# Two zero products over all 128 rows ahead of each group of 32-row merging products in a hybrid HGRN2 / RWKV-7 step

## The chip, the cores and the metric

The kernel runs on one core of a Trainium2 chip. The metric is the device time of one execution in microseconds (us); a smaller number is better. The core's engines are TensorE (PE in the profile, with its weight loads as PEld), VectorE (DVE), ScalarE (ACT), GpSimd (POOL) and SyncE (SP), which issues most of the DMAs.

## The reference

One inference step of a two-layer trunk: layer 0 is an HGRN2 mixer, layer 1 is an RWKV-7 mixer, each beside cross-attention to a memory, with a gate, an output projection and a residual. 1024 prompt tokens and 8 sequences of 8 sample tokens go through. What the change touches is the recurrence of RWKV-7:

```
def step(S, inp):
    r_t, w_t, k_t, v_t, a_t, b_t = inp
    sa = jnp.einsum('bhij,bhj->bhi', S, a_t)
    S = S * w_t[:, :, None, :] + sa[..., None] * b_t[:, :, None, :] + v_t[..., None] * k_t[:, :, None, :]
    y = jnp.einsum('bhij,bhj->bhi', S, r_t)
    return S, y
```

There are 16 heads of width 64, and everything is computed in 32-bit floating point.

## The kernel before, in words

The recurrence is computed in chunks of 64 tokens. A block (class `Blk`) holds 128 tokens of the prompt, that is two chunks (`E` = 2), or the 64 sample tokens (`E` = 1). There are eight prompt blocks and one sample block, in the order 0, sample, 1, 2, ... 7 (`RSEQ`). For a chunk and a head the feedback through `sa` is a unit triangular system of 64 rows, and its inverse is built in these steps:

- `pre` loads and scales the operands (tiles `BKz`, `AR`, `G`).
- `score` forms 64x64 tables of all heads on TensorE (tile `psc`, L1461) and VectorE writes them, masked, to `Q` (L1464).
- `inverse` solves blocks of 16 rows on VectorE, one row after another (tiles `pd` and `Xc`, L1534 and L1535).
- `merge_steps` puts the 16-row blocks together to 32 rows and these to 64 rows, by products of 32x32 matrices on TensorE (all in L1560). This is where the change is.
- `chain` carries the state from chunk to chunk (tiles `chain` and `chainS`, L1643 to L1700), and `out` normalizes and stores.

In `merge_steps` the inner function `prods` makes five steps: `pn1`, `px32`, `py32`, `pn2`, `py64` (the profile and the orders print them as `pn`, `px`, `py`, `pn`, `py`, with the operands behind the arrow). A step works on the quarters of a block, a quarter being 32 rows of one chunk. It takes two quarters at a time: a group. Each quarter of a group has a PSUM bank of its own, from the pool `psi` with two banks, and 16 products of 32x32 (one for each head) fill the bank; the two quarters alternate in the code, and an engine then copies the 32 filled rows out of the bank. `pn1` and `py32` have two groups in a prompt block, the others one: seven groups. In the sample block five groups stand, two of them with two quarters and three with one. A 32-bit product shows as two records in the profile, so a group of 32 products has 64 records. A group uses 32 rows and 32 columns of the array at a time.

The order on each engine is not the order of the code. A scheduler places each instruction by a simulated timeline, so that one added instruction can move others on every engine; `chain` stands under `tc.high_priority()`. Merging products of one block therefore lie among the chain of the block ahead of it, the scores (`psc`) of the next one, and the sample block's own work: transposes of its states (`ps`, L1602), products with them (`pas`, L1617), and their addition to the chain (L1647). `chain` already has two products of zeros of the kind that the change adds, in the first block alone (`zb`, L1643, 128 rows, 512 columns, bfloat16).

Of the kernel before, what the change touches and what calls it, by code (L numbers as in the profile page):

```python
# [906 lines left out]
def rwkv_masks(g, rc, c):  # L907

    nc = g.nc
    BF16 = mybir.dt.bfloat16  # L910
    si = c.tile([128, 64], I32, name="rsi")
    ti = c.tile([128, 64], I32, name="rti")
    xi = c.tile([128, 64], I32, name="rxi")
    nc.gpsimd.iota(si, pattern=[[0, 64]], base=0, channel_multiplier=1)
    nc.gpsimd.iota(ti, pattern=[[1, 64]], base=0, channel_multiplier=0)
    nc.vector.tensor_scalar(si, si, 63, None, op0=ALU.bitwise_and)
    nc.vector.tensor_tensor(xi, si, ti, op=ALU.bitwise_xor)
    m = g.rmask = rc.tile([128, 2, 128], F32, name="rm")
    for e in range(2):
        nc.vector.tensor_tensor(m[:, e, 64 - 64 * e:128 - 64 * e], ti, si, op=ALU.is_gt)  # L920
        nc.vector.tensor_tensor(m[:, e, 64 * e:64 * e + 64], ti, si, op=ALU.is_ge)
    b = c.tile([128, 64], F32, name="rb")
    nc.vector.tensor_scalar(b, xi, LS, None, op0=ALU.is_lt)
    g.rmask_s = rc.tile([128, 128], F32, name="rms")
    nc.vector.tensor_tensor(g.rmask_s.rearrange("p (a t) -> p a t", a=2), m[:, 0].rearrange("p (a t) -> p a t", a=2),
                            b[:, None, :].to_broadcast([128, 2, 64]), op=ALU.mult)

    g.smask = rc.tile([128, 512], BF16, name="smask")
    nc.vector.memset(g.smask, 1.0)
    nc.vector.memset(g.smask[:, 0:512:64], 0.0)  # L930
    g.smask_s = rc.tile([128, 256], BF16, name="smask_s")
    nc.vector.memset(g.smask_s, 1.0)
    nc.vector.memset(g.smask_s[:, 0:256:LS], 0.0)

    g.BKz = [rc.tile([128, 2, 4, 4, 64], F32, name=f"BKz{k}") for k in range(2)]
    for k in range(2):
        for h in range(2):
            nc.gpsimd.memset(g.BKz[k][HV[1 - h], h], 0.0)

    g.Xc = rc.tile([128, 16, 16], F32, name="Xc")  # L940
    nc.vector.memset(g.Xc, 0.0)
    nc.vector.memset(g.Xc.rearrange("p r t -> p (r t)")[:, 0:256:17], 1.0)
    g.N1p = rc.tile([128, 16, 32], F32, name="N1p")
    for q in range(4):
        s = slice(32 * q, 32 * q + 32)
        nc.vector.tensor_copy(g.N1p[s], g.ident[s, None, s].to_broadcast([32, 16, 32]))
    g.m16 = rc.tile([128, 32], I32, name="m16")
    nc.gpsimd.iota(g.m16, pattern=[[0, 32]], base=0, channel_multiplier=1)
    nc.vector.tensor_scalar(g.m16, g.m16, 16, 4, op0=ALU.bitwise_and, op1=ALU.logical_shift_right)
    g.bm = rc.tile([128, 2], F32, name="bm")  # L950
    nc.vector.tensor_copy(g.bm[:, 1:2], g.m16[:, 0:1])
    nc.vector.tensor_scalar(g.bm[:, 0:1], g.bm[:, 1:2], -1.0, 1.0, op0=ALU.mult, op1=ALU.add)
    nc.vector.memset(g.m16[:, 16:], 0)
# [19 lines left out]
def rwkv_layer(ctx, g, nn, left):  # L973
# [219 lines left out]
    with pool(g, "rtmp", 1) as tmp:  # L1193
        rwkv_masks(g, P["s"], tmp)
# [98 lines left out]
def copy(nc, eng, dst, src):  # L1293
    if eng == "scalar":
        nc.scalar.activation(dst, src, AF.Copy)
    else:
        getattr(nc, eng).tensor_copy(dst, src)
# [67 lines left out]
class Blk:  # L1365
# [179 lines left out]
    def merge_steps(self):  # L1545

        g, Q, XN, XP = self.g, self.Q, self.XN, self.XP
        nc = g.nc
        quart, un, ac = self.quart, self.un, self.ac
        XM = self.tile("XM", "XM", 16, 32)  # L1550
        N1 = g.N1p
        tl = lambda nm: g.psi.tile([128, 16, 32], F32, name=nm, tag="i")

        def prods(nm, qs, out, lhs, rhs, evac):

            for k in range(0, len(qs), 2):
                zs = [(c, tl(nm)) for c in qs[k:k + 2]]
                for u in range(16):
                    for c, z in zs:
                        nc.tensor.matmul(z[out(*c), u], lhs(u, *c), rhs(u, *c), start=True, stop=True)  # L1560
                for c, z in zs:
                    evac(z[out(*c)], *c)

        def to_q(z, e, s, c):
            for k in range(2):
                nc.scalar.activation(un(k, e, s, c), z[:, 8 * k:8 * k + 8], AF.Copy)
        Qu = lambda u, e, s, o: Q[u // 8][s, self.turn(e, u // 8), u % 8 // 4, u % 4, ac(e, o, 32)]
        same = lambda e, q, s: s
        order = [c for c in quart if c[1] == 0] + [c for c in quart if c[1] == 1]
        lo = [c for c in quart if c[1] == 0]  # L1570
        up = lambda s: slice(s.start + 32, s.stop + 32)
        prods("pn1", order, same, lambda u, e, q, s: Qu(u, e, s, 32 * q), lambda u, e, q, s: XN[s, u],
              lambda z, e, q, s: nc.vector.copy_predicated(N1[s], g.m16[s, None, :].to_broadcast([32, 16, 32]), z))
        yield
        prods("px32", lo, same, lambda u, e, q, s: XP[s, u], lambda u, e, q, s: N1[s, u],
              lambda z, e, q, s: copy(nc, ENG["xm"], XM[s], z))
        yield
        prods("py32", order, same, lambda u, e, q, s: N1[s, u], lambda u, e, q, s: XP[s, u],
              lambda z, e, q, s: to_q(z, e, s, ac(e, 32 * q, 32)))
        yield  # L1580
        prods("pn2", lo, lambda e, q, s: up(s), lambda u, e, q, s: Qu(u, e, s, 32), lambda u, e, q, s: XM[s, u],
              lambda z, e, q, s: copy(nc, ENG["xm"], XM[up(s)], z))
        yield
        prods("py64", lo, same, lambda u, e, q, s: XM[up(s), u], lambda u, e, q, s: Qu(u, e, up(s), 32),
              lambda z, e, q, s: to_q(z, e, s, ac(e, 32, 32)))
# [175 lines left out]
    def out(self, last=False):  # L1761

        for k in range(2):
            self.out_group(k, last)
# [88 lines left out]
```

## Time and profile before

| what | us |
|---|---|
| median of the 3 runs | 2386.9 (2386.75 to 2400.98) |
| the profiled execution's own time | 2401.76 |
| its span, first to last instruction | 2399.8 |
| TensorE matmul busy | 2238.2 (93%) |
| VectorE busy | 1332.2 (56%) |
| ScalarE busy | 1004.3 (42%) |
| GpSimd busy | 717.7 (30%) |

Busy time of TensorE is modelled, since matmuls are pipelined: a product's duration reaches past the start of the next one, and the distance from start to start is what a product takes of the engine. The mean granted TensorE clock was 0.934 of full speed in the profiled execution. The merging products of this program start at 1723.6 us and end at 2210 us of the span; the gate projections before them and the output projection behind them are large products. The profiled execution was as long as the slowest of the three runs.

### The profile page before, as it was taken

The page shows a single profiled execution, that of the slowest core. Times are in us where ns is not written, and L with a number is a line of the kernel's source. Part 1 is how long each engine was busy: PE and PEld are TensorE (multiplying, and loading weights), DVE is VectorE, ACT ScalarE, POOL GpSimd, SP SyncE. Part 2 cuts the span into 40 slices and gives each one's busy share as a digit, 9 for nine tenths or more (in the row PEclk, how much of TensorE's full clock was granted, in tenths as well). Part 3 has the DMA queues.
Part 4 walks back from the last instruction along what each step waited for, and adds up shares of the span by engine and source line. Part 5 has one row for each costly group of instructions (what it writes and reads, how often), then busy time and mean ns, then how long its engine had stood idle before and what let it go on. Part 6 is the DMA issues. An engine that isn't in the chain of part 4 may idle for free. (4 is left out here: it accounts for less than half of the span.)

```text
span 2399.8 us, 50625 instructions
## 1 busy us (share of the span) xinstructions
PE 2238.2 (93%) x20980; PEld 2001.5 (83%) x20981; DVE 1332.2 (56%) x2678; ACT 1004.3 (42%) x2240; POOL 717.7 (30%) x559
## 2 busy tenths in 40 slices
PE   5988999999999979989989998999999998899997
PEld 5988888888788858878979998898889987788786
DVE  6113566556775553365796214245576589874643
ACT  4222444444444442266554313344544455444421
POOL 2123121122112310034553412113143255444432
PEclk9998999999999989999999998999986798887999
DMA  5334111223432264215434425145332233312653
GB/s 184 86 96 142 48 56 45 67 70 91 111 87 87 80 193 127 84 41 199 148 122 163 127 93 145 50 103 134 113 108 72 57 101 99 90 55 82 201 158 105
DMA packets 360312, 252.99 MB, mean 105 GB/s; under 512 B 120379, under 2 KB 326403, under 8 KB 360083
## 3 DMA queue, kind: packets, MB, share of 16 engines
q1 hardware_dynamic: 348034, 237.66, 33.3%
q0 software_dynamic: 2544, 7.64, 0.9%
q10 hardware_dynamic: 9504, 4.46, 0.7%
q8 instruction: 165, 2.70, 0.5%
q14 instruction: 65, 0.52, 0.1%
HBM read 172.59 MB, written 77.11 MB: 104 GB/s over the span
## 5 line engine op out<-in xcount | busy, mean ns | idle before, releaser
L200 POOL TENSOR_TENSOR wlo<-wraw,whi 128x1024 fp32r<-128x1024 f32 (+1 forms) x84 | 214.9, 2560 | 646.5 <-ACT whi L197 623.8
L216 PE MATMUL pg<-hi,whi 128*128 128x288 f32 (+3 forms) x800 | 269.1, 336 | 4.5 <-DVE qk L597 2.3
L218 PE MATMUL pg<-hi,wlo 128*128 128x288 f32 (+3 forms) x800 | 266.0, 333 | 0.0
L217 PE MATMUL pg<-lo,whi 128*128 128x288 f32 (+3 forms) x800 | 265.9, 332 | 0.0
L197 ACT ACTIVATE whi<-wraw 128x1024 fp32r<-128x1024 f32 (+1 forms) x92 | 101.0, 1099 | 178.5 <-issue 104.9
L216 PEld LDWEIGHTS pg<-hi,whi 128*128 128x128 f32 x800 | 153.8, 192 | 21.5 <-issue 4.4
L217 PEld LDWEIGHTS pg<-lo,whi 128*128 128x128 f32 x800 | 153.7, 192 | 12.9 <-issue 3.1
L218 PEld LDWEIGHTS pg<-hi,wlo 128*128 128x128 f32 x800 | 153.5, 192 | 11.8 <-issue 2.3
L890 PE MATMUL pout<-owh,bh 128*128 128x512 f32 (+1 forms) x432 | 143.1, 397 | 9.2 <-ACT owh L197 9.2
L890 PE MATMUL pout<-owl,bh 128*128 128x512 f32 (+1 forms) x432 | 142.0, 394 | 0.1
L890 PE MATMUL pout<-owh,bl 128*128 128x512 f32 (+1 forms) x432 | 141.2, 394 | 0.9 <-DVE bl L200 0.9
L216 PE MATMUL pg<-xhi,whi 128*128 128x384 f32 (+2 forms) x392 | 127.6, 325 | 7.1 <-DVE evs L1136 5.0
L218 PE MATMUL pg<-xhi,wlo 128*128 128x384 f32 (+2 forms) x392 | 126.4, 322 | 0.0
L217 PE MATMUL pg<-xlo,whi 128*128 128x384 f32 (+2 forms) x392 | 125.5, 320 | 0.0
L1461 PE MATMUL psc<-AR,BKz 128*128 128x128 f32 x544 | 98.2, 342 | 17.2 <-DVE Q L1464 9.3
L1461 PEld LDWEIGHTS psc<-AR,BKz 128*128 128x128 f32 x544 | 86.7, 244 | 23.1 <-DVE Q L1464 11.0
L890 PEld LDWEIGHTS pout<-owh,bh 128*128 128x128 f32 (+1 forms) x432 | 78.9, 183 | 31.3 <-ACT owh L197 10.8
L197 ACT ACTIVATE bh<-br 128x512 fp32r<-128x512 f32 (+1 forms) x54 | 32.4, 606 | 171.5 <-POOL br L859 84.4
L200 DVE TENSOR_TENSOR bl<-br,bh 128x512 fp32r<-128x512 f32 (+1 forms) x54 | 49.6, 919 | 96.2 <-ACT bh L197 96.2
L890 PEld LDWEIGHTS pout<-owh,bl 128*128 128x128 f32 (+1 forms) x432 | 78.6, 182 | 22.8 <-DVE bl L200 1.8
L242 PE MATMUL pg<-xhi,wlo 128*128 128x384 f32 (+1 forms) x408 | 96.6, 334 | 0.0
L890 PEld LDWEIGHTS pout<-owl,bh 128*128 128x128 f32 (+1 forms) x432 | 78.8, 183 | 21.1 <-DVE owl L200 0.6
(460 smaller groups left out, 6114.9 us busy)
## 6 DMA issues: line engine op xcount, KB each, us to landing
wraw<-in_w_in_dram SPq DMA_DIRECT2D x72, 512.0 KB
oraw<-in_w_out_dram SPq DMA_DIRECT2D x24, 512.0 KB
wraw<-in_w_mem_kv_dram SPq DMA_DIRECT2D x16, 512.0 KB
gT<-evs SPq DMA_DIRECT2D x12, 544.0 KB
vv<-vtk SPq DMA_DIRECT2D x24, 256.0 KB
br<-brT SPq DMA_DIRECT2D x24, 256.0 KB
br<-mixT SPq DMA_DIRECT2D x24, 256.0 KB
gt<-gT SPq DMA_DIRECT2D x24, 256.0 KB
```

The source lines that it names most:

```text
L197: nc.scalar.activation(hi, src, AF.Copy)
L200: (nc.gpsimd if elo == "pool" else nc.vector).tensor_sub(lo, src, hi.bitcast(F32))
L216: nc.tensor.matmul(out, ah, bh, start=first, stop=False)
L217: nc.tensor.matmul(out, ah, bl, start=False, stop=False)
L218: nc.tensor.matmul(out, al, bh, start=False, stop=last)
L242: nc.tensor.matmul(z[:, :n], a[:, k], x(k)[:, t0:t0 + n], start=first, stop=last)
L890: nc.tensor.matmul(ps[c][:p], a[:, k, :p], w[:, 512 * c:512 * c + 512], start=first, stop=last)
L1461: nc.tensor.matmul(ps[:, j], two(BK[:, h, j, 2 * e:2 * e + 2]), two(AR[:, j, 2 * e:2 * e + 2]), start=True, stop=True)
```

## The change

A tile of 128x128 bfloat16 zeros (`zd`) is made once, in `rwkv_masks`. In `prods`, ahead of the products of a group, each bank of the group gets one product of zeros by zeros over 128 rows, 128 columns of the array and 512 columns of the moving operand, which fills the whole bank with zeros. The merging products then write their 32 rows of the bank as before (`start=True`), so what is copied out of the bank is the same.

```
@@ -919,6 +919,8 @@
         nc.vector.tensor_tensor(m[:, e, 64 * e:64 * e + 64], ti, si, op=ALU.is_ge)
+    g.zd = rc.tile([128, 128], BF16, name="zd")
+    nc.vector.memset(g.zd, 0.0)
     b = c.tile([128, 64], F32, name="rb")
@@ -1555,6 +1557,10 @@
             for k in range(0, len(qs), 2):
                 zs = [(c, tl(nm)) for c in qs[k:k + 2]]
+
+                for _, z in zs:
+                    nc.tensor.matmul(z.rearrange("p u t -> p (u t)"), g.zd, g.zd[:, None, :].to_broadcast([128, 4, 128]),
+                                     start=True, stop=True)
                 for u in range(16):
                     for c, z in zs:
                         nc.tensor.matmul(z[out(*c), u], lhs(u, *c), rhs(u, *c), start=True, stop=True)
```

In the changed program lines behind the first insertion are 2 higher and those behind the second 6 higher: the merging products are L1566 there and the zeros L1562.

The scheduler's order on TensorE in the first prompt block, before: the last half of step `pn2` (`pn<-XM,Q`) and step `py64` (`py<-Q,XM`), a number behind a tile telling one bank from another.

```order
L1560 MATMUL pn_17450<-XM,Q 32x32 x7
L1643 LDWEIGHTS zb
L1643 MATMUL chain_18180<-zb 128x512
L1560 MATMUL pn_17450<-XM,Q 32x32 x9
L1560 MATMUL pn_17451<-XM,Q 32x32 x16
L1560 MATMUL py_17486<-Q,XM 32x32 x16
L1560 MATMUL py_17487<-Q,XM 32x32 x16
L1461 MATMUL psc<-AR,BKz_15166 128x128 x8
```

The same place in the changed program:

```order
L1562 LDWEIGHTS zd
L1562 MATMUL pn_17462<-zd 128x512
L1566 MATMUL pn_17462<-XM,Q 32x32 x16
L1562 LDWEIGHTS zd
L1562 MATMUL pn_17463<-zd 128x512
L1566 MATMUL pn_17463<-XM,Q 32x32 x16
L1491 MATMUL pbk<-ident,BKz_15167 128x64 x4
L1491 MATMUL pbk<-ident,BKz_15168 128x64 x4
L1608 MATMUL ps_18365<-ident,Sn_18366 128x64 x4
L1562 LDWEIGHTS zd
L1562 MATMUL py_17500<-zd 128x512
L1566 MATMUL py_17500<-Q,XM 32x32 x16
```

The second bank's zeros stand behind the first bank's 16 products, not ahead of the group, and transposes (`pbk`, `ps`) that stood elsewhere have come between the two steps. The zeros of the chain (`zb`) have moved to an earlier place.

The second place is the sample block's step `px32` (one bank) on TensorE and what follows it, before:

```order
L1461 MATMUL psc<-AR,BKz_15166 128x128 x4
L1489 MATMUL pbk<-ident,BKz_15165 128x64 x8
L1560 MATMUL px_18870<-N1p,XP 32x32 x16
L1560 MATMUL py_18900<-XP,N1p 32x32 x16
L1647 MATMUL chain_18179<-ident,AS_18347 128x64
L1617 MATMUL pas<-AR,S0T 64x2x8 x8
```

And in the changed program:

```order
L1463 MATMUL psc<-AR,BKz_15167 128x128
L1562 LDWEIGHTS zd
L1562 MATMUL px_18888<-zd 128x512
L1566 MATMUL px_18888<-N1p,XP 32x32 x4
L1653 MATMUL chain_18195<-ident,AS_18363 128x64
L1623 MATMUL pas<-AR,S0T 64x2x8 x8
L1566 MATMUL px_18888<-N1p,XP 32x32 x12
L1463 MATMUL psc<-AR,BKz_15167 128x128 x8
```

The step is cut in two by a round of the sample block's state products, and eight score products follow where the next merging step stood.

## Rows read from the trace of the kernel before

**Rows 1.** The page: busy time of TensorE, and its granted clock in 40 slices.
```profile
PE 2238.2 (93%) x20980; PEld 2001.5 (83%) x20981; DVE 1332.2 (56%) x2678; ACT 1004.3 (42%) x2240; POOL 717.7 (30%) x559
...
PEclk9998999999999989999999998999986798887999
```
**Rows 2.** Busy time by stretch (us): span:, length, engines, PEclk, DMA share, GB/s.
```profile
1786.00:1896.00 110.00, 109.39 (x1261) 102.19 (x1262) 60.21 (x119) 47.48 (x115) 27.76 (x26) 0.57 0.24 62
1896.00:2050.00 154.00, 141.66 (x2456) 126.19 (x2453) 135.63 (x243) 76.01 (x195) 91.82 (x92) 0.92 0.36 96
2050.00:2215.00 165.00, 156.26 (x2570) 140.95 (x2570) 111.72 (x226) 77.29 (x200) 72.77 (x76) 0.82 0.24 69
1723.00:2215.00 492.00, 467.78 (x7249) 425.47 (x7247) 347.58 (x663) 229.06 (x572) 216.99 (x223) 0.81 0.30 81
```
**Rows 3.** The chain that ended last, by line, in 1786:1896 and in 1896:2050.
```profile
by line: PE psc L1461 24.4%; PE pas L1617 18.4%; PE py L1560 14.6%; PE pn L1560 10.4%; PE chain L1647 6.2%; PE pbk L1489 5.6%; PE chain L1652 5.1%; PE px L1560 5.1%; PE ps L1602 3.5%; PE chain L1677 2.5%; PE chain L1650 1.5%; PE chain L1691
...
by line: DVE pd L1534 12.1%; DVE BKz L1425 6.2%; PE chain L1650 6.2%; PE psc L1461 5.9%; DVE G L1415 5.7%; PE chain L1652 5.0%; issue 4.6%; PE chain L1677 4.1%; DVE Xc L1535 3.8%; PE pn L1560 3.6%; PE py L1560 3.6%; PE px L1560 3.4%; DVE UV
```
**Rows 4.** Windows of L1560 alone: PE and PEld busy, PEclk, DMA.
```profile
1723.00:2215.00 492.00, 137.45 (x3808) 124.99 (x3808) 0.81 0.30 81
```
**Rows 5.** TensorE in order of time: start, duration, line, tiles, count.
```profile
1742.64 1.85 PE L1560 MATMUL py<-XP,N1p 32*32 32x32 f32 x56
1744.43 0.39 PE L1643 MATMUL chain<-zb 128*128 128x512 bf16 x1
1744.75 0.31 PE L1560 MATMUL py<-XP,N1p 32*32 32x32 f32 x8
...
1746.35 0.39 PE L1643 MATMUL chain<-zb 128*128 128x512 bf16 x1
1746.67 1.60 PE L1560 MATMUL pn<-XM,Q 32*32 32x32 f32 x48
```
**Rows 6.** The chain that ended last, in order of time: output projection, 512 columns each.
```profile
2262.14 6.96 PE pout L890 x29
```
**Rows 7.** The same chain: 16 score records at either clock.
```profile
1818.47 3.71 PE psc L1461 x16
1906.62 1.98 PE psc L1461 x16
```
**Rows 8.** Who waited for whom, longest in total: merging products, 1723:2215.
```profile
PE py L1560 <- ACT XM L1295: 2.0, 1, 2.0
PE pn L1560 <- ACT Q L1566: 1.5, 2, 0.7
```
**Rows 9.** Windows of the half-clock stretches that begin behind merging products, with their sum.
```profile
1748.60:1755.40 6.80, 6.80 (x75) 6.51 (x73) 2.35 (x5) 3.22 (x9) 0.33 (x1) 0.50 0.49 130
1844.20:1895.40 51.20, 51.20 (x569) 47.91 (x567) 22.52 (x50) 18.58 (x44) 7.47 (x7) 0.50 0.25 62
...
sum 119.20, PE 113.33 PEld 106.45 DVE 60.21 ACT 42.17 POOL 29.44; mean PE 12.59 PEld 11.83 DVE 6.69 ACT 4.69 POOL 3.27
```
**Rows 10.** Windows of the other half-clock stretches, with their sum.
```profile
1786.10:1830.50 44.40, 43.89 (x425) 41.01 (x426) 29.27 (x60) 18.08 (x44) 16.32 (x14) 0.50 0.23 61
...
sum 68.30, PE 64.00 PEld 59.54 DVE 49.76 ACT 29.18 POOL 29.58; mean PE 16.00 PEld 14.88 DVE 12.44 ACT 7.30 POOL 7.39
```
**Rows 11.** Windows just ahead of two of these stretches, all engines.
```profile
1782.00:1786.00 4.00, 2.48 (x27) 2.20 (x26) 3.81 (x8) 0.79 (x2) 3.21 (x4) 1.00 0.65 184
1840.00:1844.20 4.20, 4.20 (x119) 4.05 (x112) 3.71 (x4) 4.11 (x11) 2.87 (x2) 1.00 0.08 20
```
**Rows 12.** Windows of L1560 alone ahead of such stretches, and in one stretch at full clock.
```profile
1744.40:1748.60 4.20, 2.97 (x92) 2.65 (x89) 1.00 0.81 260
1840.00:1844.20 4.20, 2.50 (x90) 2.28 (x82) 1.00 0.08 20
2099.60:2103.60 4.00, 1.92 (x58) 1.81 (x58) 1.00 0.02 5
...
1905.60:1919.20 13.60, 3.54 (x178) 3.10 (x173) 1.00 0.21 58
```

More of the change, by code (lines that the diff above doesn't have):

```diff
@@ L921, in rwkv_masks @@
         nc.vector.tensor_tensor(m[:, e, 64 * e:64 * e + 64], ti, si, op=ALU.is_ge)
+    g.zd = rc.tile([128, 128], BF16, name="zd")
+    nc.vector.memset(g.zd, 0.0)
     b = c.tile([128, 64], F32, name="rb")
@@ L1557, in prods @@
                 zs = [(c, tl(nm)) for c in qs[k:k + 2]]
+                for _, z in zs:
+                    nc.tensor.matmul(z.rearrange("p u t -> p (u t)"), g.zd, g.zd[:, None, :].to_broadcast([128, 4, 128]),
+                                     start=True, stop=True)
                 for u in range(16):
```

## The prediction

> **What bounds the kernel now.** I read first the page, for the share of the engines and the granted clock, then the stretches that hold the changed code, then the chain of waits in them. TensorE is busy for 93% of the span, and its clock is below full mostly in the last third [rows 1]. All the merging products lie between 1723 and 2215 us, a stretch of 492 us [rows 2, 4]. What stands ahead of it is, by the order, the same in both programs up to the last gate projections, and the output projection behind it does not touch the change, so I take these parts as they are.
>
> In the 492 us TensorE is busy for 467.8 us, so it idles for 24.2 us in all, and its mean clock is 0.81 [rows 2]. The reader is to see three parts. From 1786 to 1896 (the sample block between prompt blocks 0 and 1) TensorE idles for 0.6 us at a clock of 0.57, and the chain holds nothing but TensorE lines at its head: scores, state products, merging products [rows 2, 3]. From 1896 to 2050 the clock is 0.92, TensorE idles for 12.3 us, VectorE is busy for 135.6 of 154 us and heads the chain with the 16-row solves (`pd`) [rows 2, 3]. From 2050 to 2215 the clock is 0.82 and TensorE idles for 8.7 us [rows 2]. So an added product costs TensorE time nearly everywhere, and part of that is lost in VectorE's shadow in the middle part; and a higher clock would pay most in the first part.
>
> Two levels of the clock occur, full and half. Half-clock stretches add up to 119.2 + 68.3 = 187.5 us [rows 9, 10]: nine stretches, 119.2 us, begin right behind merging products (90 records in the 4.2 us before the longest one, which lasts 51.2 us, with TensorE busy throughout, and 58 before another) [rows 9, 11, 12]; four, 68.3 us, begin elsewhere, mostly where TensorE waits (2.48 us busy of the 4 before the 44.4 us one, and no merging product in it) [rows 10, 11]. Sixteen score records take 3.71 us at half clock and 1.98 us at full [rows 7], so one us at half clock that becomes full gives back 1 - 1.98/3.71 = 0.47 us, as long as TensorE is the bound.
>
> **The change: what it adds.** Seven groups of two banks in each of 8 prompt blocks are 112 products of zeros, and the sample block's five groups add 2 + 1 + 2 + 1 + 1 = 7: 119 products and as many weight loads. The 3808 records of merging products [rows 4] stay. The one memset of the zeros is nothing: it is one instruction on VectorE while TensorE works through the gate projections.
>
> The price of one at full clock is read at two places. The trace has two products of the very same shape among merging products. The merging row of 56 begins at 1742.64 and its starts are 0.032 us apart; the zeros start at 1744.43 and the next merging product at 1744.75; the second time it is 1746.35 and 1746.67 [rows 5]. That is 0.32 us from the zeros to the next product, and with the gap ahead of them (the last merging start is near 1744.30) 0.45 us, less the 0.03 of an ordinary step: 0.42 us. Where 512-column products follow one another, 29 take 6.96 us: 0.24 us each [rows 6]. In the changed order 42 of the 119 stand between two merging products, the second bank's zeros behind the first bank's products, as the first of the two places in the order shows; 77 stand behind something else, mostly products over many rows. So 42 x 0.42 + 77 x 0.24 = 17.6 + 18.5 = 36.1 us of TensorE at full clock. At half clock no row shows this shape; I scale by the scores, 0.24 x 3.71/1.98 = 0.45, so 0.21 us more. If 30% of the zeros run there, it is 36 x 0.21 = 7.5 us.
>
> What hides them: the zeros need a free bank but not the operands, so they can run while TensorE waits. In front of merging products that is little, 2.0 + 1.5 us [rows 8]; in the stretch as a whole it is the 24.2 us of idle time. I take half of it, 12 us, since TensorE's waits in the middle part are for scores and the chain, whose turn is not always next to a group. Cost: 36.1 + 7.5 - 12 = about 31 us. The bounds are 119 x 0.24 - 24.2 = 4 us and 119 x 0.42 + 7.5 = 57 us.
>
> **The change: what it may give back.** The zeros put full-height work among the merging products. For this speaks the stretch from 1905.6 to 1919.2: 178 merging records in it, with chain and score products between them, and the clock stays at 1.00 [rows 12]. Against it speaks the place that is nearest to the changed kernel: from 1744.4 to 1748.6 there are 92 merging records with the two products of zeros among them, and the clock falls to half right behind, at 1748.6 [rows 5, 9, 12]. The changed order has one product of zeros for 32 records instead of one for 46, so it is denser than that, though not by much. I take it that a third of the 119.2 us that begin behind merging products stays at full clock, 40 us, and nothing of the 68.3 us: 40 x 0.47 = 19 us. The bounds are nothing and 119.2 x 0.47 = 56 us; everything at full clock would be 187.5 x 0.47 = 88 us, which VectorE, busy for 60.2 of the 110 us [rows 2] and for most of the middle part, would not allow.
>
> By the Trainium skill ("TensorE: Matmul & The Clock Gate", section "Why this matters for your kernels") drops of the clock are avoided by leaving no idle gaps between bursts of matmuls. By that the busy merging stretches should not lose the clock at all, and zeros among them would give back nothing, which would make the sum 2387 + 31 = 2418. The trace does not agree with it for small products: TensorE is busy for 109.39 of 110 us at a clock of 0.57 [rows 2].
>
> **The change: what it moves.** On TensorE the groups break up more (the second place in the order: the sample block's `px32` is cut by a round of state products), but more products alternate between two banks in the changed order, 641 against 592, which costs less per product; I count the two as nothing. Scores and the sample block's state loads and products stand in another order between 1760 and 1900 us, and I see no wait that this removes or adds for certain; it goes into the range with 10 us either way.
>
> **The sum.** The profiled execution takes 2401.8 us, 14.9 above the median of 2386.9; the change makes it 2401.8 + 31 - 19 = 2414, and carried to the median 2386.9 + 12 = **2399 us**, 0.5% slower.
>
> **The rivals.** *The clock comes back in the sample block's part.* In the changed order eight score products, of full height, follow where merging products stood, so the 51.2 us stretch, and part of the 44.4 us one, may stay at full clock. This decides from 31/0.47 = 66 us of regained clock (no change) and gives more than 1% faster from (31 + 24)/0.47 = 117 us. With all of 51.2 + 44.4 = 95.6 us and a third of the other 68 us that begin behind merging products: 118 us x 0.47 = 56 us, so 2387 + 31 - 56 = 2362. For it speaks that TensorE alone is on the chain there [rows 3]; against it that the 44.4 us begin with a wait, not with merging products [rows 11]. *The clock does not come back at all,* as behind 1748.6: a product of zeros is too small a part of a group, TensorE is the bound, and each one is paid: 2387 + 31 = 2418, and 2430 if nothing is hidden. This one ends clearly slower; it decides where less than 15 us of half clock is regained ((31 - 24)/0.47). *The change does not do what it says:* the scheduler does not put two zeros ahead of a group but splits the pair, so that most stand between merging products at 0.42 instead of 0.24 us: 119 x 0.42 = 50, 14 more than in the sum, 2413. Against it: 77 of 119 have other work ahead.
>
> **How the numbers follow.** About 1%, 24 us, is what a measurement of this kernel can tell from no change; the three runs alone spread over 14 us. My forecast, 2363 to 2411, gets 0.53. The regained sample part gets 0.15 (2340 to 2362). No regained clock gets 0.24 (2411 to 2440), and the split pairs 0.08, half of it under 2411. So faster 0.15, same 0.57, slower 0.28. The range that leaves 2 in 10 out reaches to both sides: 2360 to 2430. The forecast's own is 2375 to 2411.
>
> **What would show it.** Right: L1562 with 119 products on TensorE, their cost read from the start before to the start behind them near 0.42 and 0.24 us; the half-clock time between 1723 us and the output projection near 150 us instead of 187.5; TensorE's idle time there under 24 us; VectorE's busy time unchanged. Wrong towards faster: a clock near 0.9 in the sample block's part. Wrong towards slower: a clock of 0.81 or less in the whole stretch with TensorE busy time up by over 30 us. It would also be wrong if the moved order, not the zeros, set the time: a new wait on TensorE's scores or chain of over 10 us.

## The result and the profile after

| | median us | lowest to highest | runs |
|---|---|---|---|
| before | 2393.3 | 2386.8 to 2401.0 | 4 |
| after | 2419.3 | 2414.9 to 2423.1 | 4 |

The ratio is 1.0107, 95% interval 1.0062 to 1.0152: 26 us slower. The forecast was 2399 us, and its range, 2360 to 2430, holds the result. The direction was right, the size less than half of what came.

The page of the kernel after: TensorE, its clock in 40 slices, and VectorE.

```profile
span 2413.0 us, 50822 instructions
PE 2266.0 (94%) x21099; PEld 1999.9 (83%) x21100; DVE 1326.2 (55%) x2679; ACT 1004.8 (42%) x2240; POOL 717.6 (30%) x559
PEclk8999999999999989999999999999867799997999
```

TensorE is busy for 27.8 us more than in [rows 1], VectorE for 6.0 us less: the added work is TensorE's alone. The windows of the same three stretches as [rows 2] (us; then busy us and count of PE, PEld, DVE, ACT, POOL; the granted clock; DMA share; GB/s):

```profile
1786.00:1896.00 110.00, 109.64 (x1220) 96.98 (x1219) 62.77 (x124) 48.45 (x117) 31.62 (x31) 0.65 0.28 72
1896.00:2050.00 154.00, 151.43 (x2528) 126.56 (x2527) 126.94 (x236) 75.97 (x194) 86.78 (x89) 0.95 0.34 90
2050.00:2215.00 165.00, 159.57 (x2573) 132.76 (x2572) 111.75 (x228) 73.71 (x194) 73.29 (x76) 0.91 0.22 60
```

The clock rose from 0.57, 0.92 and 0.82 [rows 2] to 0.65, 0.95 and 0.91. These are the same times, not the same work: from the first merging product to the last state product the profile after runs from 1715.7 to 2245.4 us, the one before from 1723.6 to 2231.6. The half-clock stretches from 1736 us on, first, longest and sum:

```profile
1736.60:1760.50 23.90, 23.90 (x261) 19.95 (x259) 10.99 (x22) 9.62 (x25) 8.21 (x6) 0.50 0.29 73
...
1859.50:1897.00 37.50, 37.50 (x421) 31.38 (x420) 17.74 (x46) 15.47 (x38) 7.34 (x8) 0.50 0.23 59
...
sum 167.10, PE 165.66 PEld 142.24 DVE 81.08 ACT 65.44 POOL 55.59; mean PE 12.74 PEld 10.94 DVE 6.24 ACT 5.03 POOL 4.28
```

The zeros are there as the change says, as the view of L1562 shows (duration in ns: least, median, most; first and last start):

```profile
L1562 PEld LDWEIGHTS <-zd x119: 95/97/206, 1693.0 to 2213.2; 128*128 128x128 bf16 x119
L1562 PE MATMUL pn<-zd x51: 379/389/609, 1693.0 to 2208.5; 128*128 128x512 bf16 x51
L1562 PE MATMUL py<-zd x51: 376/389/634, 1730.7 to 2213.2; 128*128 128x512 bf16 x51
L1562 PE MATMUL px<-zd x17: 376/390/609, 1726.5 to 2190.6; 128*128 128x512 bf16 x17
```

What one costs is read from the starts, in TensorE's order of time. At full clock, one behind a score, one behind a chain product and one between two merging products (start, then duration):

```profile
1942.83 0.28 PE L1463 MATMUL psc<-AR,BKz 128*128 128x128 f32 x1
1942.94 0.38 PE L1562 MATMUL pn<-zd 128*128 128x512 bf16 x1
1943.25 1.19 PE L1566 MATMUL pn<-XM,Q 32*32 32x32 f32 x32
...
1945.92 0.39 PE L1562 MATMUL py<-zd 128*128 128x512 bf16 x1
1946.24 0.43 PE L1566 MATMUL py<-Q,XM 32*32 32x32 f32 x8
1946.60 0.39 PE L1562 MATMUL py<-zd 128*128 128x512 bf16 x1
1946.92 1.19 PE L1566 MATMUL py<-Q,XM 32*32 32x32 f32 x56
```

From a zero to the merging product behind it is 0.31 to 0.32 us. At half clock it is 0.54 and 0.53 us:

```profile
1862.25 0.61 PE L1562 MATMUL px<-zd 128*128 128x512 bf16 x1
1862.79 1.91 PE L1566 MATMUL px<-N1p,XP 32*32 32x32 f32 x32
1864.64 0.61 PE L1562 MATMUL px<-zd 128*128 128x512 bf16 x1
1865.17 0.95 PE L1566 MATMUL px<-N1p,XP 32*32 32x32 f32 x14
```

**A measure for the comparisons.** In every kernel below I take the stretch from the first merging product to the end of the last state product; its window shows its length and TensorE's busy time. Before, after and two of the experiments (doubled zeros, then alternation alone) read:

```profile
1723.60:2231.60 508.00, 479.87 (x7444) 436.56 (x7444) 357.93 (x680) 238.41 (x590) 226.74 (x232) 0.82 0.31 84
```
```profile
1715.70:2245.40 529.70, 508.97 (x7542) 434.25 (x7542) 358.64 (x689) 238.16 (x595) 230.55 (x236) 0.85 0.30 82
```
```profile
1727.20:2240.90 513.70, 492.50 (x7660) 402.73 (x7659) 361.57 (x689) 238.48 (x595) 230.64 (x236) 0.94 0.31 85
```
```profile
1722.50:2206.50 484.00, 436.30 (x7448) 389.08 (x7448) 358.29 (x680) 239.11 (x597) 227.20 (x233) 0.86 0.33 90
```

From the stretch's length I take 0.47 us [rows 7] for each us of half clock in it. What is left is its length at full clock: 508.0 - 0.47 x 187.7 = 419.8 us before, 529.7 - 0.47 x 163.8 = 452.7 us after. One profile's half-clock time isn't exact to the us: ahead of 1700 us, where the programs are the same, it lies between 105.8 and 122.9 us in these profiles. And the profiled execution of before is itself 8 us over its median, with a mean granted clock of 0.934 where 53 runs of before have 0.931 to 0.942 and 0.936 on average: its half-clock time is rather long.

Two figures from all runs, not from one profile, stand beside the table. Each run has its mean granted clock, shown in the column "clock"; twice what it lacks of 1, times the span, is the run's half-clock time. That is 304 us for the runs of before on average, 285 for the changed kernel, 208 for e4_double, 305 for e9_low2 and 262 for e6_alt. And over the runs of before, one us of half clock goes with 0.37 us of time (fitted within each of their three series), so 0.47, read from the scores alone, may be too much: the step between merging records falls from 0.053 us at half clock to 0.031 at full (medians, changed kernel), which gives back 0.42. At 0.37 the last column would show the changed kernel 30.5 us above before instead of 32.9, and the doubled zeros 52.4 us instead of 65.0.

| run | median us | against before, 95% interval | clock | stretch | TensorE idle | half clock | at full clock |
|---|---|---|---|---|---|---|---|
| before | 2393.3 | | 0.936 | 508.0 | 28.1 | 187.7 | 419.8 |
| after | 2419.3 | 1.006 to 1.015 | 0.941 | 529.7 | 20.7 | 163.8 | 452.7 |
| e1_tiny | 2397.4 | 1.000 to 1.004 | 0.936 | 513.7 | 28.0 | 198.0 | 420.6 |
| e2_narrow | 2412.5 | 1.006 to 1.010 | 0.936 | 516.1 | 26.9 | 170.7 | 435.9 |
| e3_low | 2409.8 | 1.005 to 1.009 | 0.939 | 521.0 | 26.3 | 167.3 | 442.4 |
| e5_keep | 2429.8 | 1.012 to 1.017 | 0.940 | 545.1 | 20.2 | 180.9 | 460.1 |
| e8_one | 2409.0 | 1.006 to 1.011 | 0.940 | 516.9 | 30.7 | 157.0 | 443.1 |
| e4_double | 2408.4 | 1.005 to 1.011 | 0.957 | 513.7 | 21.2 | 61.4 | 484.8 |
| e9_low2 | 2431.7 | 1.014 to 1.020 | 0.937 | 542.3 | 18.6 | 177.5 | 458.9 |
| e6_alt | 2373.9 | 0.991 to 0.996 | 0.945 | 484.0 | 47.7 | 136.5 | 419.8 |
| e7_altz | 2390.1 | 0.997 to 1.001 | 0.945 | 498.9 | 34.4 | 139.9 | 433.1 |
| e10_altz2 | 2387.4 | 0.997 to 1.001 | 0.958 | 492.5 | 26.1 | 78.5 | 455.6 |
| e11_part | 2373.5 | 0.991 to 0.995 | 0.948 | 478.8 | 44.7 | 112.6 | 425.9 |

### The profile page after: what moved, and what is told of

It reads as the page before. It is cut to its first block, busy times and chain, and to the rows that moved or that the text cites. A ratio compares the mean times of both kernels' runs of the same rounds, so it can differ in the third digit from the quotient of the medians.

```text
span 2413.0 us, 50822 instructions
## 1 busy us (share of the span) xinstructions
PE 2266.0 (94%) x21099; PEld 1999.9 (83%) x21100; DVE 1326.2 (55%) x2679; ACT 1004.8 (42%) x2240; POOL 717.6 (30%) x559
## 5 line engine op out<-in xcount | busy, mean ns | idle before, releaser
L242 PE MATMUL pg<-xhi,whi 128*128 128x384 f32 (+1 forms) x408 | 95.0, 332 | 0.0
L242 PE MATMUL pg<-xlo,whi 128*128 128x384 f32 (+1 forms) x408 | 93.9, 330 | 0.0
```

Of the source, the lines that this page charges most:

```text
L242: nc.tensor.matmul(z[:, :n], a[:, k], x(k)[:, t0:t0 + n], start=first, stop=last)
```

## The experiments

The theory (A): the loss is the time of the zeros themselves, exposed on TensorE, less a small part that comes back as clock; the moved order adds nothing. Rivals: the moved order makes the loss; the clock gives nothing back, or would give it all with more of the same work. The diffs below tell which instructions are changed, in words; only that of e6_alt is source.

**Only the order (e1_tiny).** In the finished program, order and waits as they are, each zero product and its load are cut to one 32-row tile:

```diff
-zd[128 rows, 128 columns of weights], 512 columns -> z[128 rows, 512]
+zd[32 rows, 32 columns of weights], 32 columns -> z[32 rows, 32], tile of the first merging product behind it
```

> The changed kernel's order on every engine, with each of the 119 zero products cut to 32 rows by 32 columns of one 32-row tile (the loads too), so that it costs no more than one merging product; the result is not touched, since every word of the banks is written again. Theory A (the zeros' own TensorE time makes the 26 us, the moved order nothing): 119 x about 0.03 = 4 us, so 2393 + 4 = 2397 (2391 to 2402), and half-clock time near the 195 us of before. Rival B (the moved order costs by itself, 10 us or more, and the zeros only what was predicted or less): 2404 to 2419. Rival C (the moved order itself helps, by the clock or by alternation, and the zeros cost more than the 38 us read so far): under 2391.

2397.4 us, 5.7 over the 2393.0 of before by the ratio, with 0.8 us more at full clock. That is A's number: the moved order by itself costs nothing that can be told from the tiny products' own 4 us. The 22 us from here to the changed kernel are the zeros' size.

**Height without columns (e2_narrow).** All 128 rows and all weights, but 32 columns:

```diff
-moving: zd, 128 rows x 512 columns
+moving: zd, 128 rows x 32 columns
```

> The changed kernel's order, each zero product over all 128 rows with all of its 128 columns of weights, but 32 columns moving instead of 512. Theory A: what stays is the change between 32-row tiles and the whole array, 0.42 - 0.24 = 0.18 us for those between merging products plus about 0.06 to 0.1 us for each of the 119: 42 x 0.18 + 119 x 0.08 = 17 us, no clock given back, so about 2410 (2402 to 2415). If the columns are all that costs, 2393 to 2400 (the narrow product is then nearly free). If the change of tile with its load of weights is all that costs, 2412 to 2420, as the whole change. If height alone, without columns, gives clock back: half-clock time between 1700 and 2250 us under 175 us, and a time under 2400.

2412.5 us, 0.76% over before: 70% of the loss with a sixteenth of the columns. At full clock it adds 16.1 us, against 17 expected. The starts show why, TensorE in order of time at full clock:

```profile
1981.47 0.18 PE L1562 MATMUL py<-zd 128*128 128x32 bf16 x1
1981.58 0.88 PE L1566 MATMUL py<-XP,N1p 32*32 32x32 f32 x22
1982.39 0.19 PE L1562 MATMUL py<-zd 128*128 128x32 bf16 x1
1982.51 0.94 PE L1566 MATMUL py<-XP,N1p 32*32 32x32 f32 x26
```

Over the kernel, at full clock, the next merging product begins 0.119 us behind the narrow one (median of 78), and the narrow one begins 0.123 us behind a merging product (median of 26), where merging products follow one another in 0.031. Narrow ones behind narrow ones take 0.039 (five of them). So each change between the whole array and a 32x32 tile costs about 0.09 us. It is the same with 512 columns: in the changed kernel a merging product begins 0.319 us behind a zero (median of 76), another zero 0.227 (median of five). The Trainium skill ("TensorEngine Tiling (Array Packing)", section "Key Properties") has it that a change of the tiling mode, not of the tile alone, drains TensorE; the runs agree that such a change costs, and give it this price. That the cost is a drain no run here shows.

**Columns without height (e3_low).** 512 columns in one 32-row tile:

```diff
-zd[128 rows, 128 columns of weights], 512 columns -> z[128 rows, 512]
+zd[32 rows, 32 columns of weights], 512 columns -> z[32 rows, 512], same tile as the merging product
```

> The changed kernel's order, each zero product 512 columns wide but in one 32-row tile (weights 32 x 32), the tile of the first merging product behind it. Theory A: the columns, 119 x 0.24 = 29 us at full clock and up to 45 at half, without the 42 x 0.18 = 8 us for the change of tile, and no clock given back since nothing is full-height: 2393 + 29 to 40 = 2422 to 2433, half-clock time near 195 us or more. If products in other 32-row tiles go on beside it, half of it is hidden: 2405 to 2412. Rival (columns in one tile give as much clock back as full height): half-clock time near 165 us and 2410.

2409.8 us and 22.6 us more at full clock: under the 29 of the columns. TensorE in order of time shows why, at full clock, behind a chain product and behind a merging product:

```profile
1898.17 0.39 PE L1562 MATMUL pn<-zd 32*32 32x512 bf16 x1
1898.40 0.47 PE L1566 MATMUL pn<-XN,Q 32*32 32x32 f32 x10
...
1916.30 0.38 PE L1562 MATMUL px<-zd 32*32 32x512 bf16 x1
1916.32 0.93 PE L1566 MATMUL px<-N1p,XP 32*32 32x32 f32 x21
```

In the first place the next merging record begins 0.23 us behind the low zero (so in 52 of 77 at full clock). In the second, three records begin within 0.09 us of it and the fourth at 0.226 (25 of 77): part of its columns is hidden by merging products beside it. The half-clock time of 167 us speaks for the rival, but one profile can be off by that much; the doubled run below decides.

**The zeros in the order of before (e5_keep).** The program of before, with a zero product put into the finished order ahead of each bank's first product (the last two banks' ahead of the ordering):

```diff
+load zd (128 x 128)
+z[128 rows, 512] = zd x zd, with the waits of the product behind it
 first merging product into z
```

> The order of the kernel before, exact up to the middle of the last prompt block on TensorE, with a zero product (128 rows, 512 columns, and its load of weights) put right ahead of the first merging product of each of the 119 banks, which hands its waits to it; 60 of them stand between two merging products. Theory A (the zeros' own time, order nothing): 60 x 0.42 + 59 x 0.24 = 39 us at full clock, less what is given back, as in the changed kernel or a little more since the zeros here wait for the operands too: 2417 to 2428. Rival B (the moved order costs 10 us or more): 2398 to 2410. Rival C (the moved order helped by 10 us or more): 2429 to 2440.

2429.8 us, 40.3 us more at full clock against 39 expected. It is 10 us slower than the changed kernel by the medians (the two intervals overlap). Of the 7.4 us at full clock between the two, some 3 are explained by place (60 instead of 42 between merging products, 18 x (0.41 - 0.24)); the rest, that these zeros wait for operands too, was not tried by itself. So rival B is out; a mild form of C, that the moved order helped by some us, is likely but not shown.

**Half the zeros (e8_one).** The second zero of a pair is cut to one tile as in e1_tiny; 61 full ones stay.

> The changed kernel's order, a full zero product for the first bank of each pair and of each single bank (61), the other 58 cut to 32 rows by 32 columns of one 32-row tile. These first ones stand mostly behind other work. Theory A (each product pays for itself, by its place): of the 33 us that the 119 add at full clock, 61 x 0.24 = 15 us less a part of TensorE's waits, so 8 to 15, and half as much clock given back (5 us): 2397 + 3 to 10 = 2400 to 2407. If cost goes by the number alone: 2397 + 22 x 61/119 = 2408. Rival (one full-height product for each group gives back as much clock as two): half-clock time near 165 us in 1700 to 2250 and a time no longer than that of the tiny ones, 2392 to 2398.

2409.0 us, the number of "cost goes by the number alone". At full clock it adds 23.3 us, more than the 8 to 15 I took: the first of a pair isn't the cheap one.

**Twice the zeros (e4_double).** Each zero and its load are issued twice:

```diff
 load zd; z = zd x zd
+load zd; z = zd x zd
```

> The changed kernel's order with each zero product, its load of weights too, issued twice in a row into the same bank: 238 products. Theory A: the second one follows a product of 512 columns, so 119 x 0.24 = 29 us at full clock, 5 more where the clock is half, and what TensorE can still hide is used up; given back another 10 us at most: 2419 + 34 - 10 = 2443 (2433 to 2455), half-clock time in 1700 to 2250 us near 145. Rival (the clock is held once there is enough full-height work): half-clock time under 80 us, 2419 + 29 - 40 = 2408, or less. Rival (nothing is given back by zeros, and the 29 us less half-clock time were chance): half-clock time 165 to 205, 2450 to 2460.

2408.4 us, 0.8% over before where the single ones were 1.1% over it: 11 us under them by the medians (the two intervals overlap), and 35 us under the 2443 of my own theory, which falls in its second half. At full clock it adds 65.0 us, twice the 32.9 of the single ones (52.4 against 30.5 if a us of half clock is worth 0.37); from the starts, 119 x 0.23 = 27 us more were to come. But the half-clock time fell to 61 us, and the rival had 2408. Its half-clock stretches, two of the eight and the sum:

```profile
1861.70:1878.80 17.10, 17.10 (x171) 12.88 (x167) 9.60 (x33) 3.82 (x10) 2.61 (x3) 0.50 0.45 118
...
2199.60:2216.70 17.10, 17.10 (x191) 12.92 (x189) 2.29 (x8) 7.17 (x19) 4.32 (x3) 0.50 0.38 109
...
sum 64.80, PE 64.18 PEld 52.19 DVE 28.28 ACT 21.65 POOL 13.98; mean PE 8.02 PEld 6.52 DVE 3.53 ACT 2.71 POOL 1.75
```

By these profiles doubling gave back 102 us of half clock where the first set gave 24; by the clocks of all runs it is 77 (285 to 208) and 19 (304 to 285).

**Twice the columns, low (e9_low2).** e3_low's products, each twice:

> The changed kernel's order with each zero product cut to one 32-row tile (512 columns, weights 32 x 32) and issued twice. The single low ones add 22.6 us at full clock to the stretch of the merging products, the second set should add as much. If the clock is held by work over all 128 rows, which these lack: half-clock time in 1700 to 2250 us stays at 160 to 195 us, and the time is 2410 + 23 = 2433 (2425 to 2440). If it is held by columns that move, whatever the height (as with the doubled full ones, half-clock time 65 us): 2410 + 23 - 49 = 2384 (2378 to 2395). In between: height and columns both count.

2431.7 us, the number that was expected if the half-clock time stays. Half-clock stretches, longest and sum:

```profile
1862.60:1900.20 37.60, 37.60 (x418) 31.57 (x414) 18.19 (x47) 14.27 (x35) 5.20 (x6) 0.50 0.25 64
...
sum 177.70, PE 176.54 PEld 152.56 DVE 87.70 ACT 72.07 POOL 54.08; mean PE 12.61 PEld 10.90 DVE 6.26 ACT 5.15 POOL 3.86
```

The same number of products and the same columns as in e4_double, in the same order, in 32 rows instead of 128: 177.7 instead of 64.8 us of half clock, with TensorE busy for 176.5 us of them. All six runs of each say the same: granted clock 0.951 to 0.961 in e4_double, 0.932 to 0.943 here. So with the doubled products over the whole array the clock mostly stood at full, and with the same moving columns in one 32x32 tile it did not; nor does the absence of gaps explain it. These products have fewer rows and also fewer columns of weights, 32 instead of 128; which of the two matters was not tried.

**Alternation without zeros (e6_alt).** On before; the same line on the changed kernel is e7_altz:

```diff
-nc.tensor.matmul(z[out(*c), u], lhs(u, *c), rhs(u, *c), start=True, stop=True)
+x = nc.tensor.matmul(z[out(*c), u], lhs(u, *c), rhs(u, *c), start=True, stop=True)
+if (u, c) != (0, zs[0][0]):
+    g.tc.keep_in_program_order(x)
```

> No zero products: the kernel before, with the products of a pair of banks held in the order in which the program writes them, so that they alternate between the two banks: 1744 of 1904 products stand behind one of the other bank instead of 592. Products that alternate start 0.019 us apart for each of their two records, those of one bank 0.032: 1152 x 2 x 0.013 = 30 us at full clock, so 2393 - 30 = 2363 (2355 to 2375) if this is TensorE time on the path. Rival: a group that is held together shuts out the scores and chain products that stood in its gaps, and VectorE and TensorE wait for one another: idle time of TensorE up by 15 us or more, 2378 to 2395. Rival: the denser groups lose the clock for longer (half-clock time over 215 us): 2370 to 2385.

2373.9 us, 0.67% faster than before and the first version that beats both. TensorE's busy time in the stretch falls by 43.6 us, but its idle time rises from 28.1 to 47.7 us, so both the saving and the first rival's new waits are real; they cancel at full clock (419.8 in both), and the gain is half-clock time: 51 us less in this profile, and 43 us less by the clocks of all runs (0.943 to 0.947 in the six), which at 0.37 to 0.47 is 16 to 20 us, the whole gain. The longest of the new waits, in the view of who waits for whom over the stretch (us in total, times, longest):

```profile
PE chainS L1702 <- DVE UV L1685: 7.7, 5, 1.9
PE chain L1693 <- DVE UV L1685: 5.2, 3, 2.3
PE py L1560 <- ACT XM L1295: 4.6, 7, 2.0
```

TensorE now waits for the chain's evacuations (`UV`); in the kernel before the same two waits are 1.2 and 0.3 us in the stretch. Why the clock is better here, where nothing over 128 rows was added, is not settled.

> The changed kernel, zeros as they are, with the products of a pair of banks held in the order in which the program writes them: 1699 products alternate instead of 641, 38 zeros between two merging products instead of 42. Theory A (zeros cost their own time whatever the order, alternation saves its own): 2419 - 1058 x 2 x 0.013 = 2419 - 27 = 2392, that is 26 us above the same order without zeros. Rival (zeros earn more where the groups are dense): within 10 us of the same order without zeros.

2390.1 us, a little under theory A's 2392, and 16 us above the same order without zeros, between A's 26 and the rival's 10: with 34.4 us of idle time left against 47.7 without them, 13 us of them are hidden in the new waits.

**Doubled zeros with alternation (e10_altz2, e11_part).** e7_altz with each zero twice, and the same with only the first 35 doubled and the other 84 cut to one tile:

> The products of a pair of banks held in the order in which the program writes them, and every full zero product with its load issued twice. Against the same with single zeros (2390): 33 us more at full clock, and if the clock is held as in the doubled run before (half-clock time 143 to about 60 us, 83 x 0.47 = 39 us given back): 2384 (2375 to 2390), no better than alternation alone (2374), since the zeros cost about what they bring back. If TensorE's 34 us of waits in this order hide more of them: 2365 to 2375. If the clock is not held: 2415 to 2425.

> As the run with alternation and doubled zeros, but only the first 35 zero products (up to about 1900 us, where half of the half-clock time lies) are full and doubled, and the other 84 are cut to 32 rows by 32 columns in one tile. Cost 70 x 0.28 = 20 us at full clock; given back, if the clock is held up to 1900 us, 82 to about 25 us of half clock, 57 x 0.47 = 27 us: 2374 + 3 + 20 - 27 = 2370 (2362 to 2380), that is no clear gain over alternation alone. If the clock up to 1900 us is not held: 2390 to 2400.

2387.4 and 2373.5 us, the first 3 us above its expected 2384, the second 3.5 above its 2370. Half-clock time goes down with the number of doubled zeros (139.9, 78.5; 112.6 us with the part), and their time at full clock takes it back. Neither is better than alternation alone by what can be measured.

## Why the prediction was right in direction and half in size

**What bounds.** Right: in the stretch the changed kernel's TensorE is idle for 20.7 of 529.7 us, and VectorE's busy time is the same (358.6 and 357.9 us).

**The price of one.** Right between merging products: 0.123 us from the last merging start and 0.32 to the next, less 0.03, is 0.41 (0.42 predicted), 42 times as the order said. Too low for a part of the other 77, which I took at 0.24 as standing behind "products over many rows". Behind a score it is 0.11 + 0.31 less the 0.205 us that the step from a score to a merging product took before (median of 5): 0.22, some 32 times with the other products over the whole array. Behind the 64-row or 64-column products of chain and sample state, some 40 times, it is 0.154 + 0.32 - 0.152 (median of 34 before) = 0.32: a zero there is a second change of the tile. 42 x 0.41 + 32 x 0.22 + 40 x 0.32 + 5 x 0.23 (zero behind zero) = 38.2 us instead of 36.1.

**What hides them.** This term was mis-sized: 12 us taken, half of the idle time; idle time fell by 28.1 - 20.7 = 7.4 us. Together the two make 30.8 us at full clock; measured are 32.9 (30.5 at 0.37), and predicted were 24.1.

**What the clock does.** Predicted were 7.5 us for the zeros at half clock less 19 us given back: -11.5. Measured is half-clock time down by 23.9 us: 23.9 x 0.47 = -11.2. The parts fit, too: 31 of the 119 ran at half clock (30% taken), 31 x 0.54 = 17 us of half clock that are the zeros' own, so some 40 us of the old came back; but no run separates these, and the half-clock time that I named for the profile, 150 us, forgot the zeros' own. By the clocks of all runs the half-clock time fell by 19 us, not 24, which is 7 to 9 us of time: the profile of before had more of it than most runs.

**The sum.** So the profile's stretch is 32.9 - 11.2 = 21.7 us longer, where the sum had 24.1 - 11.5 = 12: the step that failed is the cost at full clock, by the cover of 12 us, of which 7.4 came, and by one price for all places that are not between merging products. The remaining 4 us to the 26 of the medians are within what the two profiled executions differ from theirs: with the 7 to 9 us given back over all runs, the 26 us are 33 to 35 us of cost at full clock.

**The rivals.** That the clock is not regained at all gave 2418, the number nearest to the result, for a reason that is wrong: half-clock time did fall, and with twice the zeros it falls to a third. By the Trainium skill ("TensorE: Matmul & The Clock Gate", section "Why this matters for your kernels") it is idle gaps between bursts that lose the clock; here the trace disagrees once more, since e9_low2 has 177.7 us of half clock with TensorE busy for 176.5 of them, and e4_double, with more idle time in the stretch (21.2 against 18.6 us), has 61.4. The regained sample part: the clock there rose from 0.57 to 0.65, not to 0.9. Split pairs: 42 zeros stand between merging products, as the order had it, and not 119. The moved order: with tiny products in it (e1_tiny) it costs nothing of its own.

**The step behind the give-back.** I took it as a share of the stretches, a third. The runs show that it does not grow evenly with the zeros: none (e1_tiny), 61, 119 and 238 full zeros leave 198, 157, 164 and 61 us of half clock, at mean clocks of 0.936, 0.940, 0.941 and 0.957 over all runs. From 61 to 119 nothing comes back that can be told, from 119 to 238 most of it does. The changed kernel thus stands where the zeros are paid and the clock is still lost.

## What to carry to other kernels

Price an inserted product by its neighbours: where they run in another tile of the array, the change there and back is paid with every one, here about half of what the zeros cost at full clock (16.1 of 32.9 us). If work is added to hold the clock, try two doses before judging: cost grew by a similar amount with each (33, then 65 us; 31, then 52 at the lower worth of half clock), most of the clock came back only with the second, and both doses were slower than none. And look first at the order of what is there: letting two banks' products alternate brought 0.7%, which no filler did.

## What the runs showed of the hardware

- A change between the whole array and a 32x32 tile costs TensorE about 0.09 us each way at full clock (narrow product: 0.123 us to its start and 0.119 from it, against 0.031 between merging products and 0.039 between narrow ones).
- Among the same merging products the granted clock stood at half for 177.7 us with doubled filler of 512 columns in one 32x32 tile (e9_low2), and for 64.8 us with filler of as many columns over the whole array (e4_double). Rows and columns of weights were not cut apart.
- The same code ahead of 1700 us had between 105.8 and 122.9 us of half clock in single executions; at 0.47 us each that is 8 us. Over whole executions of the kernel before, the mean granted clock lay between 0.931 and 0.942, and the longer runs were mostly those at the lower clock (0.37 us for each us of half clock).
- A 512-column product in one 32x32 tile let three records of merging products begin within 0.09 us of it (25 places in e3_low), where one over the whole array let the next begin only 0.319 us behind it.
